# Halves of the last block, the first cast behind a high part, and an offset piece of attention in a hybrid decoder layer

## The chip, the cores and the metric

The kernel runs on one core of a Trainium2 chip. The metric is the device time in microseconds of one execution. The kernel before took 2251.83 us, the median of three runs (2251.02, 2251.83 and 2252.1). The engines are called PE (TensorE, matrix products; PEld is its weight load), ACT (ScalarE), DVE (VectorE), POOL (GpSimd) and SP (SyncE, which here issues most of the DMAs). "L417" is line 417 of the kernel before.

## The reference, cut to what matters

One layer on 256 tokens of width 2048: a SwiGLU feed-forward, a mixer of windowed attention beside RWKV-7 time mixing, a cross-attention into a memory, a second feed-forward, and a last RMS norm.

```
x = x + 0.5 * swiglu(rms_norm(x, ffn1_norm), ffn1_w_gate, ffn1_w_up, ffn1_w_down)
x = gated_parallel_mixer(x, mix_norm, w_in, sinks, ..., w_proj_attn, w_proj_rwkv, w_out)
x = memory_cross_attention(x, mem, cross_norm, mem_norm, w_q, w_kv, w_o)
x = x + 0.5 * swiglu(rms_norm(x, ffn2_norm), ffn2_w_gate, ffn2_w_up, ffn2_w_down)
return rms_norm(x, final_norm)

def rms_norm(x, g):          # mean over the 2048 columns of a token
    return x * rsqrt(mean(x * x) + 1e-6) * g
def swiglu(h, w_gate, w_up, w_down):
    return (silu(h @ w_gate) * (h @ w_up)) @ w_down
```

The windowed attention has 16 heads of 64 in 4 groups that share a key and a value head. The 256 tokens are two blocks of 128; the queries of a block see their own block and the one before it, within a window of 128. Each head has a sink, which takes part in the maximum and in the sum of the softmax alone.

## The kernel before, in words

All products are taken in about full float precision out of three passes in fp32r: an operand is divided into a high part (a cast on ACT) and a low part (the rest, a subtraction on DVE), and `times` (L414) adds high x high (L417), high x low (L418) and low x high (L419) in one PSUM bank. Weights come in units of 256 rows by 512 columns. `load` (L321) fetches them, through SP's queue but for one piece, `split_unit` (L338) casts (L344) and subtracts (L345), two units ahead of their use (`AHEAD`), in buffers of three.

Activations stand with features across partitions. `feat` (L598) transposes a block of token rows on PE into one of the two "tr" banks of PSUM (L605). `Norm.block` (L625) takes these transposes, multiplies them by the gain into the high part (ACT, L632) and makes the low part (DVE, L633). The factor of the norm is applied after the product. It is a square with a sum per token on ACT (L641, and L1528 for the last norm), then in `rstd` (L648) a reduction and a scaling on DVE (L651, L652) and a power on POOL (L654).

The order of the work is a list of generators, `Interleave` (L52). The main products run as plain loops (`product`, L395, and `product_pair`, L477), and after each piece of a product they call `bg.tick()`, which advances the background generators by one step each, at most `limit` of them in a group. So attention, norms and the RWKV chain are woven between the main products; `yield from idle(n)` lets n steps pass. What comes out is then put in an order for each engine by a scheduler of the framework, which may move an instruction past others where no dependency forbids it; `tc.issue_after(i)` adds an edge that keeps the instructions under it behind `i` on its engine.

**Start.** The rows of x and the first weights are issued at once; the very first weight is fetched in pieces. The first two units (u < AHEAD) are cast in halves, and `tc.issue_after(first.ins)` (L343) keeps these casts behind `first`, the copy of the first gain (L252, L265).

**Attention.** `attend(kv, qb)` (L835) is one piece: four query heads of one key head, and one block of 128 queries. It waits for the keys, makes four scores in two "mm" banks out of a ring of three (L844), scales and masks them on DVE (L850), takes the maximum (L857) and the sink, the exponentials on ACT with their sums (L869), the division on DVE (L877), transposes (L883) with copies to SBUF (L886), the product with the values (L891), and the two parts of the result (L898, L899). Scores and value products are fp32 products, which the trace records twice each. The eight pieces are put in the group "attn" (L905 to L907) in the order of kv, and of qb within it; two of the group advance at a time, the next one when one of them is done. So both blocks of a key head go in step. When the last piece is done, "attn" is set, and `decay_and_rate` (L946) starts behind it, then `removal_keys` (L1008), `substitute` (L1075), and the state's chain `pairs` (L1203) and `finish` (L1323), whose result is wanted by the product with `w_proj_rwkv` (L1398). Square roots (L1023) and the sigmoids of the gates (L1109) need different function tables on ACT.

**Tail.** The last down products of the second feed-forward are made one block of 512 columns at a time (L709 to L717). For block 3, `product(..., skew=True)` finishes the first 128 tokens some products before the others. Each result is added to x on DVE for all 512 columns (L713), then `done2` (L1525) squares and sums it on ACT (L1528) into column n of `ss`, a tile of four columns for each half of the tokens. For blocks 0 to 2, POOL multiplies by the final gain beforehand. Then, per token half, `rstd`, four scalings on ACT and DVE (L1542 to L1546) and three stores (L1549).

`aligned(sp)` (L734) takes a tile of 16 columns, "shift", at the start of each pool, and nothing uses it.

Of the kernel before, what the change touches and what calls it, by code (L numbers as in the profile page):

```python
# [7 lines left out]
F32 = mybir.dt.float32  # L8
F32R = mybir.dt.float32r
AF = mybir.ActivationFunctionType  # L10
ALU = mybir.AluOpType
# [4 lines left out]
P = 128  # L16
# [18 lines left out]
AHEAD, LOADED = 2, 4  # L35
# [97 lines left out]
def decoder_layer(ctx: ExitStack, tc: tile.TileContext, a: dict, out: bass.AP):  # L133
    nc = tc.nc
    act, dve, pool, pe = nc.scalar, nc.vector, nc.gpsimd, nc.tensor
# [4 lines left out]
    stat = ctx.enter_context(tc.tile_pool(name="stat", bufs=3))  # L140
# [23 lines left out]
    def wait_for(name):  # L164
        while name not in bg.seen:
            yield

    def idle(n):
        for _ in range(n):
            yield  # L170
# [91 lines left out]

    g_ffn1, fetch, fill = row_vectors(chunks(["ffn1_norm"], KD), "g_ffn1", act)
    fetch()
    first = fill()  # L265
    rows = chunks(["mix_norm", "cross_norm", "mem_norm", "ffn2_norm"], KD)
    gains, fetch_gains, fill_gains = row_vectors(rows, "gains", pool)
    g_mix, g_cross, g_mem, g_ffn2 = (gains[:, i * KD : (i + 1) * KD] for i in range(4))
# [69 lines left out]
    def split_unit(u, rows=slice(0, KU)):  # L338
        n, raw = units[u][3], raws[u]
        hi = wp.tile([P, KU, n], F32R, tag="hi", name="hi")  # L340
        lo = wp.tile([P, KU, n], F32R, tag="lo", name="lo")
        for s in (slice(0, 1), slice(1, 2)) if u < AHEAD else (rows,):
            with tc.issue_after(first.ins) if u < AHEAD else nullcontext():  # L343
                at["hi"] = act.copy(hi[:, s], raw[:, s])  # L344
            at["lo"] = dve.tensor_tensor(lo[:, s], raw[:, s], f32(hi[:, s]), ALU.subtract)  # L345
        return hi, lo
# [268 lines left out]
    class Norm:  # L615
# [9 lines left out]
        def block(self, n, src):  # L625

            for h in range(2):
                b = feat(src, [2 * h * P, (2 * h + 1) * P])
                for j in range(2):
                    c = 4 * n + 2 * h + j  # L630
                    g = self.gain[:, c : c + 1]
                    last = act.activation(self.x.at(0, c), b[:, j, :], AF.Copy, scale=g)  # L632
                    dve.scalar_tensor_tensor(  # L633
                        self.x.at(1, c), b[:, j, :], g, f32(self.x.at(0, c)),
                        ALU.mult, ALU.subtract,
                    )
                    self.x.done.add(c)
                yield
            with tc.issue_after(last.ins):
                for t in range(2):  # L640
                    act.activation(  # L641
                        junk_t[:], src[:, t, :], AF.Square, accum_out=self.ss[:, t, n : n + 1]
                    )
            if n == 3:
                yield
                self.r = rstd(self.ss[:])
# [11 lines left out]
    def feed_forward(sp, x, norm: Norm, wg, wu, wd, done, begin_last=lambda: None, last=False):  # L658
        if last:
            for tag, shape, dt, bufs in (  # L660
                ("hhi", [P, 16, T], F32R, 1), ("hlo", [P, 16, T], F32R, 1),
                ("hb", [P, 2, 512], F32, 2), ("thia", [P, KU, 512], F32R, 1),
                ("tloa", [P, KU, 512], F32R, 1), ("thib", [P, KU, 512], F32R, 1),
                ("tlob", [P, KU, 512], F32R, 1),
            ):
                sp.tile(shape, dt, tag=tag, name=tag, bufs=bufs)
        begun = at["item"]
        c = combinations(
            sp, norm.x, SEVEN, "c", lambda: norm.r is not None and at["item"] > begun + 4
        )  # L670
        c["next"] = []
        for gi, (j0, nj) in enumerate(GROUPS):
            h = Act(
                [sp.tile([P, 16, T], F32R, tag="hhi", name="hhi")],
                [sp.tile([P, 16, T], F32R, tag="hlo", name="hlo")], 16,
            )
            ch = combinations(sp, h, SEVEN_DOWN[nj < 4], "d", early=False)

            def transposed(hb, c):
                for q in range(2):  # L680
                    split(h, c + 2 * q, 2, feat(hb, [2 * q * P, (2 * q + 1) * P]))
                    yield

            for j in range(j0, j0 + nj):
                if j > 0:
                    hb = gate_and_up(sp, norm.x, c, norm.r, wg)

                    c["next"].append(transposed(hb, 4 * (j - j0)))
                    continue
                pg = product(norm.x, wg)  # L690
                hb = sp.tile([P, 2, 512], F32, tag="hb", name="hb", bufs=2)
                for t in range(2):
                    act.activation(hb[:, t, :], pg[t][:], AF.Silu, scale=norm.r[t])
                pu = product(norm.x, wu)
                for t in range(2):
                    dve.scalar_tensor_tensor(
                        hb[:, t, :], pu[t][:], norm.r[t], hb[:, t, :], ALU.mult, ALU.mult
                    )
                c["next"].append(transposed(hb, 0))
            end = gi == len(GROUPS) - 1  # L700
            bg.spawn("feat", c["next"].pop())
            if end:
                begin_last()

            def col(t, n):
                return x[:, t, n * 512 : (n + 1) * 512]

            for n in (0, 2):
                if last and end and n:  # L709
                    for m in (n, n + 1):  # L710
                        pd = product(h, wd, skew=m == 3)
                        for t in range(2):
                            dve.scalar_tensor_tensor(  # L713
                                col(t, m), pd[t][:], 0.5, col(t, m), ALU.mult, ALU.add
                            )
                        done(m)
                    continue  # L717
                down(sp, h, ch, wd, [[col(t, n + i) for i in range(2)] for t in range(2)])
                if end:
                    done(n)  # L720
                    done(n + 1)
# [11 lines left out]

    def aligned(sp):  # L734

        sp.tile([P, 16], F32, name="shift")


    with tc.tile_pool(name="f1", bufs=1, reuse_waits="tile") as sp:
# [4 lines left out]
        def col(n):  # L744
            return x[:, :, n * 512 : (n + 1) * 512]
# [26 lines left out]
    with tc.tile_pool(name="mx", bufs=1, reuse_waits="tile") as sp:  # L772
# [61 lines left out]

        def attend(kv, qb):  # L835
            yield from wait_for("kv")
            w = P * (qb + 1)
            tq = slice(qb * P, qb * P + P)
            s = t4("s", (P, 2, 2, T))
# [656 lines left out]


    with tc.tile_pool(name="f2", bufs=1, reuse_waits="tile") as sp:
        aligned(sp)
        at["pool"] = sp  # L1500
        x = sp.tile([P, 2, D], F32, name="x")
        fins = []

        def fin(n):

            return fins[n // 2][:, n % 2]

        def gain():
            for n in range(4):
                if n % 2 == 0:  # L1510
                    fins.append(wp.tile([P, KU, 512], F32, tag="raw", name="raw", bufs=4))
                cb = slice(n * 512, (n + 1) * 512)
                pool.dma_start(fin(n), a["final_norm"][cb].unsqueeze(0).broadcast_to([P, 512]))
                yield

        def reload():
            for n in range(4):
                cb = slice(n * 512, (n + 1) * 512)
                yield from idle(20)
                pool.dma_start(x[:, :, cb], blk(x3d, n))  # L1520

        bg.spawn("const", reload())
        ss = stat.tile([P, 2, 4], F32, tag="ss", name="ss")

        def done2(n):  # L1525
            for t in range(2):
                xs = x[:, t, n * 512 : (n + 1) * 512]
                act.activation(junk_t[:], xs, AF.Square, accum_out=ss[:, t, n : n + 1])  # L1528
                if n < 3:
                    pool.tensor_tensor(xs, xs, fin(n), ALU.mult)  # L1530

        feed_forward(
            sp, x, n4, W["ffn2_w_gate"], W["ffn2_w_up"], W["ffn2_w_down"], done2,
            begin_last=lambda: bg.spawn("const", gain()), last=True,
        )
        for t in range(2):
            r = rstd(ss[:, t : t + 1, :])[0]
            for n in range(4):
                cb = slice(n * 512, (n + 1) * 512)
                xs = x[:, t, cb]  # L1540
                if n == 3:
                    dve.scalar_tensor_tensor(xs, xs, r, fin(n), ALU.mult, ALU.mult)  # L1542
                elif n == 1:
                    dve.tensor_scalar(xs, xs, r, None, ALU.mult)
                else:
                    act.activation(xs, xs, AF.Copy, scale=r)  # L1546
            for cb, queue in ((slice(0, 1024), nc.sync), (slice(1024, 1536), act),
                              (slice(1536, 2048), nc.sync)):
                queue.dma_start(out[0, t * P : (t + 1) * P, cb], x[:, t, cb])  # L1549
# [30 lines left out]
```

## Time and profile before

| | us |
|---|---|
| median of three runs | 2251.83 |
| the profiled execution | 2252.57 |
| its span, first to last instruction | 2250.8 |
| PE idle in the span | 15.6 |
| ACT busy | 1226.5 |
| DVE busy | 1782.0 |

The profile is one execution. A row of its timeline gives the start, the duration, the engine, the line and the operation, what it writes and reads, and how many were merged (x2); in square brackets the engine's idle time ahead of it and what ended it. Products are pipelined on PE, so the time between two starts tells more than a duration. A row of the waits gives the engine and the line that waited, for whom, the sum, the number of times and the longest.

### The profile page before, as it was taken

Reading aid. Unit: us, or ns where it says so; the run is one execution under the profiler, and the core shown is the slowest. Engines: PE = TensorE matmul, PEld = TensorE weight load, DVE = VectorE, ACT = ScalarE, POOL = GpSimd, SP = SyncE. Lnnn points to the kernel's source line nnn. Section 1 sums busy time; section 2 is a strip of 40 time slices with the busy share of each in tenths; the row PEclk is TensorE's granted clock in tenths of the full one; section 3 lists DMA queues with packets and bytes.
Section 4 is the critical chain, followed back from the end, with each engine's and each line's share of the span. In section 5 each row is a group of like instructions: output and inputs, shape, how many; then the busy total and the mean of one; then the engine's idle time right before and its main releaser. Section 6 shows DMA issues by size and latency. Waiting matters only on the chain.

```text
span 2250.8 us, 28046 instructions
## 1 busy us (share of the span) xinstructions
PE 2235.2 (99%) x10617; PEld 1840.3 (82%) x10617; DVE 1782.0 (79%) x2279; ACT 1226.5 (54%) x1601; POOL 132.6 (6%) x192
## 2 busy tenths in 40 slices
PE   9999999999999999999999999999999999999998
PEld 7888888888888877788888888888888888888886
DVE  7898988998989476887534566557998988998987
ACT  6555555555556467444444446556555555554554
POOL 1000000000001000301220040001000000000002
PEclk9999999999999999999999999999999999999999
DMA  7555555556556544676523476548565565555564
GB/s 263 187 201 201 197 203 202 193 190 216 192 188 205 163 142 150 201 223 212 166 77 109 163 261 227 186 159 284 185 213 187 195 210 194 190 209 200 189 207 147
DMA packets 219143, 432.49 MB, mean 192 GB/s; under 512 B 14107, under 2 KB 16384, under 8 KB 219008
## 3 DMA queue, kind: packets, MB, share of 16 engines
q1 hardware_dynamic: 210432, 404.78, 53.3%
q0 software_dynamic: 8112, 25.12, 3.5%
q8 instruction: 83, 1.36, 0.2%
q10 hardware_dynamic: 464, 0.79, 0.1%
q14 instruction: 52, 0.43, 0.1%
HBM read 417.56 MB, written 13.11 MB: 191 GB/s over the span
## 4 chain that ended last, share of the span: by engine, by line
PE 94%; DVE 3%; DMA 1%; issue 1%; POOL 1%; ACT 0%; SPq 0%; POOLq 0%; DVEq 0%; ACTq 0%
PE acc L417 19%; PE acc L418 19%; PE acc L419 19%; PE mm L419 8%; PE mm L418 8%; PE mm L417 8%; PE tr L605 2%; PE tr L418 2%; PE tr L419 2%; PE tr L417 2%; PE mm L1254 1%; DVE lo L345 1%; PE tr L1190 1%; DMA raw<-in_w_out_dram 0%; PE mm L844 0%
## 5 line engine op out<-in xcount | busy, mean ns | idle before, releaser
L345 DVE TENSOR_TENSOR lo<-raw,hi 128x1024 fp32r<-128x1024 f32 (+1 forms) x770 | 894.5, 1163 | 336.6 <-ACT hi L344 334.4
L344 ACT CAST hi<-raw 128x1024 fp32r<-128x1024 f32 (+1 forms) x770 | 759.3, 997 | 734.7 <-PE acc L419 519.6
L417 PE MATMUL acc<-hi,xhi 128*128 128x512 f32 (+1 forms) x1196 | 474.3, 397 | 2.4 <-ACT xhi L632 1.9
L418 PE MATMUL acc<-lo,xhi 128*128 128x512 f32 (+1 forms) x1196 | 464.8, 389 | 0.0
L419 PE MATMUL acc<-hi,xlo 128*128 128x512 f32 (+1 forms) x1196 | 464.1, 388 | 0.0
L417 PEld LDWEIGHTS acc<-hi,xhi 128*128 128x128 f32 x1196 | 225.0, 188 | 51.4 <-issue 4.0
L419 PEld LDWEIGHTS acc<-hi,xlo 128*128 128x128 f32 x1196 | 224.5, 188 | 46.9 <-DVE xlo L633 1.0
L418 PEld LDWEIGHTS acc<-lo,xhi 128*128 128x128 f32 x1196 | 224.9, 188 | 45.3 <-issue 1.7
L352 ACT CAST thi<-raw 128x1024 fp32r<-128x1024 f32 x172 | 178.9, 1050 | 60.4 <-DVE raw L373 46.5
L353 DVE TENSOR_TENSOR tlo<-raw,thi 128x1024 fp32r<-128x1024 f32 x172 | 208.3, 1220 | 0.7 <-ACT thi L352 0.4
L417 PE MATMUL mm<-hi,xhi 128*128 128x512 f32 x380 | 149.3, 393 | 0.0
L419 PE MATMUL mm<-hi,xlo 128*128 128x512 f32 x380 | 148.2, 390 | 0.0
L418 PE MATMUL mm<-lo,xhi 128*128 128x512 f32 x380 | 148.2, 390 | 0.0
L418 PE MATMUL acc<-lo,hhi 128*128 128x512 f32 x372 | 145.6, 391 | 0.8 <-DVE lo L345 0.8
L419 PE MATMUL acc<-hi,hlo 128*128 128x512 f32 x372 | 145.6, 391 | 0.0
L417 PE MATMUL acc<-hi,hhi 128*128 128x512 f32 x372 | 144.9, 390 | 0.0
L419 PEld LDWEIGHTS mm<-hi,xlo 128*128 128x128 f32 x380 | 71.3, 188 | 14.8
L418 PEld LDWEIGHTS mm<-lo,xhi 128*128 128x128 f32 x380 | 71.4, 188 | 14.5
L417 PEld LDWEIGHTS mm<-hi,xhi 128*128 128x128 f32 x380 | 71.4, 188 | 14.5
L418 PEld LDWEIGHTS acc<-lo,hhi 128*128 128x128 f32 x372 | 69.9, 188 | 15.5 <-DVE lo L345 1.2
L417 PEld LDWEIGHTS acc<-hi,hhi 128*128 128x128 f32 x372 | 69.9, 188 | 14.3
L419 PEld LDWEIGHTS acc<-hi,hlo 128*128 128x128 f32 x372 | 69.9, 188 | 14.0
(392 smaller groups left out, 3511.9 us busy)
## 6 DMA issues: line engine op xcount, KB each, us to landing
raw<-in_ffn_w_up_dram SPq DMA_DIRECT2D x88, 1024.0 KB, 5.4
raw<-in_ffn_w_down_dram SPq DMA_DIRECT2D x88, 1024.0 KB, 5.1
raw<-in_ffn_w_gate_dram SPq DMA_DIRECT2D x84, 1024.0 KB, 5.1
raw<-in_w_in_dram SPq DMA_DIRECT2D x136, 512.0 KB, 3.5
raw<-in_w_out_dram SPq DMA_DIRECT2D x32, 512.0 KB, 4.5
raw<-in_w_proj_attn_dram SPq DMA_DIRECT2D x16, 512.0 KB, 3.9
raw<-in_w_proj_rwkv_dram SPq DMA_DIRECT2D x16, 512.0 KB, 5.7
raw<-in_w_cross_kv_dram SPq DMA_DIRECT2D x16, 512.0 KB, 3.6
```

The source lines that it names most:

```text
L344: at["hi"] = act.copy(hi[:, s], raw[:, s])
L345: at["lo"] = dve.tensor_tensor(lo[:, s], raw[:, s], f32(hi[:, s]), ALU.subtract)
L352: act.copy(hi[:], v[:])
L353: dve.tensor_tensor(lo[:], v[:], f32(hi[:]), ALU.subtract)
L417: pe.matmul(o, xh, hi, start=first, stop=False, **how)
L418: pe.matmul(o, xh, lo, start=False, stop=False, **how)
L419: pe.matmul(o, xl, hi, start=False, stop=last, **how)
L605: pe.transpose(b[:, o : o + P], tok[:, t, col : col + P], ident[:])
L1190: pe.matmul(b[e][:, o : o + P], x1[r, j, cs_], x2[r, j, cs_], start=True, stop=True)
L1254: pe.matmul(vb[:, (o + k) * P : (o + k + 1) * P][:, r], lhs(k, e), rhs[:, k, r], start=first and k + e == 0, stop=True, **ek,)
```

## The change

There are three edits.

1. The casts of the first two weight units are kept behind the first high part of x (`at["xhi"]`, set by the first `Norm.block`) and no longer behind the copy of the gain.
2. `attend(0, 1)` lets four steps pass before it begins. Since two pieces advance at a time and each piece is followed by the next of the list, the second lane of the attention stands four steps behind the first from there on.
3. In the last block the addition is made in two halves of 256 columns for each half of the tokens, and each half is squared at once: the first on ACT as before, the second on DVE, by an operation that multiplies and sums. The sums go to five columns, which now lie in the tile "shift" (called `room`); the fifth takes the sum of DVE.

```diff
-    first = fill()
+    fill()
...
-            with tc.issue_after(first.ins) if u < AHEAD else nullcontext():
+            with tc.issue_after(at["xhi"].ins) if u < AHEAD else nullcontext():
...
                     last = act.activation(self.x.at(0, c), b[:, j, :], AF.Copy, scale=g)
+                    at.setdefault("xhi", last)
...
                 if last and end and n:
+
+                    whole = [(t, slice(0, 512)) for t in range(2)]
+                    parts_ = [(t, slice(c, c + 256)) for t in range(2) for c in (0, 256)]
+                    pieces = {2: whole, 3: parts_}
                     for m in (n, n + 1):
                         pd = product(h, wd, skew=m == 3)
-                        for t in range(2):
+                        for t, cs in pieces[m]:
                             dve.scalar_tensor_tensor(
-                                col(t, m), pd[t][:], 0.5, col(t, m), ALU.mult, ALU.add
+                                col(t, m)[:, cs], pd[t][:, cs], 0.5, col(t, m)[:, cs],
+                                ALU.mult, ALU.add,
                             )
-                        done(m)
+                            done(m, t, cs)
...
-        sp.tile([P, 16], F32, name="shift")
+        return sp.tile([P, 16], F32, name="shift")
...
             yield from wait_for("kv")
+            if kv == 0 and qb:
+                yield from idle(4)
...
-        aligned(sp)
+        room = aligned(sp)
...
-        ss = stat.tile([P, 2, 4], F32, tag="ss", name="ss")
-
-        def done2(n):
-            for t in range(2):
-                xs = x[:, t, n * 512 : (n + 1) * 512]
-                act.activation(junk_t[:], xs, AF.Square, accum_out=ss[:, t, n : n + 1])
+        ss = room[:, :10].rearrange("p (t n) -> p t n", t=2)
+
+        def done2(n, t=None, cs=slice(0, 512)):
+            for t in range(2) if t is None else (t,):
+                xs = x[:, t, n * 512 : (n + 1) * 512][:, cs]
+                if cs.start:
+                    dve.scalar_tensor_tensor(
+                        junk_t[:, cs], xs, 1.0, xs, ALU.mult, ALU.mult, accum_out=ss[:, t, 4:5]
+                    )
+                else:
+                    act.activation(
+                        junk_t[:, cs], xs, AF.Square, accum_out=ss[:, t, n : n + 1]
+                    )
                 if n < 3:
                     pool.tensor_tensor(xs, xs, fin(n), ALU.mult)
```

## The prediction

> **What bounds the kernel now.** I read the page's span and its chain of waits first, then the busy times by stretch, then what TensorE (PE) waits for.
>
> ```profile
> span 2250.8 us, 28046 instructions
> PE 2235.2 (99%) x10617; PEld 1840.3 (82%) x10617; DVE 1782.0 (79%) x2279; ACT 1226.5 (54%) x1601; POOL 132.6 (6%) x192
> PE 94%; DVE 3%; DMA 1%; issue 1%; POOL 1%; ACT 0%; SPq 0%; POOLq 0%; DVEq 0%; ACTq 0%
> ...
> 0.00:25.00 25.00, 22.02 (x103) 17.58 (x104) 12.78 (x20) 16.37 (x32) 1.14 (x11) 1.00 0.94 337
> 2230.00:2251.00 21.00, 12.33 (x55) 9.89 (x53) 8.60 (x13) 6.22 (x10) 1.89 (x3) 0.87 0.26 100
> ```
>
> The rows by stretch give the stretch, its length, then the busy time of PE, weight load, DVE, ACT and POOL. PE is busy for 2235.2 of 2250.8 us, and 94% of the chain that ended last is PE. Its idle time is 15.6 us in all: 3.0 (25.00-22.02) in the first 25 us, 8.7 (21.00-12.33) in the last 21, and some 4 between. The three edits sit in just these places (start, attention around 787 to 850, tail). The diff takes no matmul away, so even a perfect result could not win more than a few us; nearly all of those 8.7 and 3.0 us are load and store latency that no edit touches.
>
> The profiled execution took 2252.57 us, 1.77 outside its span; the median of the three shown is 2251.83, so 0.74 is taken off a sum made against the profiled one.
>
> **Start: the first cast goes behind a high part.**
>
> ```profile
> 5.44 1.47 PE L605 MATMUL tr<-ident,x 128*128 128x128 f32 x8
> 6.88 0.62 ACT L344 CAST hi<-raw 128x512 fp32r<-128x512 f32 x1 [1.20 <-DMA raw<-in_ffn_w_gate_dram]
> 7.41 0.47 ACT L632 ACTIVATE xhi<-tr,g_ffn 128x256 fp32r<-128x256 f32 x1
> ...
> 7.92 0.19 PEld L417 LDWEIGHTS acc<-hi,xhi 128*128 128x128 f32 x1 [1.26 <-ACT xhi L632]
> ...
> 10.86 1.04 ACT L344 CAST hi<-raw 128x1024 fp32r<-128x1024 f32 x1 [1.08 <-DMA raw<-in_ffn_w_gate_dram]
> 12.33 0.50 PE L417 MATMUL acc<-hi,xhi 128*128 128x512 f32 x1 [0.91 <-ACT xhi L632]
> ```
>
> ScalarE (ACT) waits 1.20 us for the weights to land at 6.88, casts them, and only then makes the first high part, for which PE waits until 7.92. In the new order the high part comes first, inside those 1.20 us: all eight transposes are issued by 6.91 and four of them are enough for it; I put their end near 6.2, half of 1.47 behind 5.44, and its own 0.47 (L632 writes 256 columns) fits before or just behind 6.88. The cast starts at 6.88 and ends at 7.50, so the first matmul can start near 7.54: 0.4 earlier than 7.92. But what is late next is already in the trace. After its first twelve products PE waits again until 12.33, for a high part that stands on ACT behind the cast of the second weight, and this cast waits for a DMA that lands at 10.86. In the built order these two stand exactly where they stood, and the DMAs before them are the same. The 0.4 us turn into a longer wait at 12.33: I take **0**, with ends -0.4 and 0. The added wait (the cast behind the high part) holds casts and their subtractions queued on ACT and VectorE (DVE); the DMA covers it.
>
> **Attention: one piece four steps behind.** Two pieces of the attention run beside the main products, one for each 128-row block. Before, both are issued in the same step; now the second is offset by four steps, and as later pieces follow in the two lanes, the offset stays.
>
> ```profile
> PE tr L605 <- ACT tok L788: 0.8, 1, 0.8
> PE tr L605 <- DVE yalo L899: 0.3, 1, 0.3
> PE mm L844 <- DVE s L850: 0.2, 1, 0.2
> ...
> 815.01 0.40 PE L419 MATMUL acc<-hi,xlo 128*128 128x512 f32 x1
> 816.16 0.33 PE L605 MATMUL tr<-ident,tok 128*128 128x128 f32 x1 [0.75 <-ACT tok L788]
> ...
> 821.21 0.40 PE L419 MATMUL acc<-hi,xlo 128*128 128x512 f32 x1
> 821.88 0.44 PE L605 MATMUL tr<-ident,tok 128*128 128x128 f32 x2 [0.27 <-DVE yalo L899]
> ```
>
> Those are all the waits of PE between 780 and 870. Read by starts (a main product follows its forerunner by 0.23 us, below), the first two hold PE 1.15-0.23 = 0.92 and 0.67-0.23 = 0.44 us; with the 0.2 of the third that is 1.56. All come of both pieces standing together: four score products want a fourth PSUM buffer of a ring of three; a transpose wants a token tile whose scaling stands on ACT behind three copies of both pieces. Spread out, the pieces ask for two buffers at a time. I take **-1.4**: the first and third wait go, some 0.15 of the second is left. Ends: 0 (waits reappear elsewhere) and -1.56.
>
> What spreading costs is seen where an fp32 run breaks into the main products (fp32r):
>
> ```profile
> 856.56 0.39 PE L418 MATMUL acc<-lo,xhi 128*128 128x512 f32 x1
> 856.78 0.39 PE L419 MATMUL acc<-hi,xlo 128*128 128x512 f32 x1
> 857.10 1.13 PE L964 MATMUL mm<-xs,wa 64*128 64x256 f32 x8
> 858.16 0.50 PE L417 MATMUL acc<-hi,xhi 128*128 128x512 f32 x1
> 858.50 0.40 PE L418 MATMUL acc<-lo,xhi 128*128 128x512 f32 x1
> ...
> 795.70 0.71 PE L844 MATMUL mm<-kd,qt 64*128 64x128 f32 x6
> 796.34 0.44 PE L883 MATMUL tr<-ident,s 128*128 128x128 f32 x2
> 796.71 0.48 PE L844 MATMUL mm<-kd,qt 64*128 64x128 f32 x2
> 797.12 0.44 PE L883 MATMUL tr<-ident,s 128*128 128x128 f32 x2
> ```
>
> Main products start 0.23 apart; the one ahead of the fp32 run takes 0.32, the one behind it 0.34: 0.20 for going in and out. Inside the run there may be as much again: one fp32 matmul (two records) alone takes 797.12-796.71 = 0.41, in a run of three 0.64/3 = 0.21. In the built order the fp32 runs rise from 77 to 84, since pieces that stood together now stand apart, and the mixer steps behind the attention shift with them. Seven more at 0.20 are **+1.4**. Ends: 0 (runs broken by transposes alone, as the second fence shows, may already pay this) and 7 x 0.40 = +2.8.
>
> The end of the attention, and with it decay, removal keys, substitution and the chain of the state, come later by up to some tens of instructions. On SyncE's queue (SP) the four loads of the triangular blocks (L1080) move behind three weight loads; on GpSimd's (POOL) the loads of L950 and L951 pass one subtraction, and the gate stores (L1113) change places with the block stores (L1070). No DMA is added. Who needs the end of it is far off:
>
> ```profile
> L611 DVE TENSOR_TENSOR yrlo<-yq,yrhi x4: 684/686/693, 1186.0 to 1273.0; 128x512 fp32r<-128x512 f32 x4
> ...
> L417 PEld LDWEIGHTS acc<-hi,yrhi x64: 187/188/190, 1293.1 to 1338.8; 128*128 128x128 f32 x64
> ```
>
> The last part is ready by 1273.7 and used at 1293.1: 19.4 us. In the built order the last chain matmul stands 24 main products later, 24 x 0.23 = 5.5 us. **0**; without that cover the price is what it is late by.
>
> ACT gets two more table loads (19 for 17), since square roots now fall on both sides of a gate's sigmoid.
>
> ```profile
> 888.95 1.28 ACT L1023 ACT_TABLE_LOAD   x1
> 890.24 0.60 ACT L1023 ACTIVATE sq<-tr 128x512 f32<-128x512 f32 x1
> 891.51 1.05 ACT L344 CAST hi<-raw 128x1024 fp32r<-128x1024 f32 x1 [0.67 <-PE acc L419]
> 894.23 1.05 ACT L344 CAST hi<-raw 128x1024 fp32r<-128x1024 f32 x1 [1.67 <-PE acc L419]
> ```
>
> Behind such a load on ACT wait the casts of the weights, and behind these PE. A cast is due every 2.72 us, when PE leaves a buffer of three, so its result is wanted two units (5.44 us) later; cast (1.05) and subtraction (1.23, below) leave about 3.1 us. The densest place issues sigmoid, load, root, load, sigmoid: 0.63+1.28+0.60+1.28+0.63 = 4.4 us, and begins about 2 us before the next cast is due. So it is some 2.4 late of 3.1: **0**. Ends: 0 and 2 x 1.28 = +2.6.
>
> [...]
>
> **Tail: the last block in halves.**
>
> ```profile
> 2242.37 0.69 DVE L713 SCALAR_TENSOR_TENSOR x<-acc,x 128x512 f32<-128x512 f32 x1 [0.30 <-PE acc L419]
> 2243.09 0.63 ACT L1528 ACTIVATE junk<-x 128x512 bf16<-128x512 f32 x1 [0.84 <-DVE x L713]
> 2243.63 0.19 ACT L1528 ACTIVATION_READ_ACCUMULATOR junk<-x 128x1 f32 x1
> 2243.84 0.16 DVE L651 TENSOR_REDUCE ms<-ss 128x1 f32<-128x4 f32 x1 [0.79 <-ACT junk L1528]
> 2244.04 0.15 DVE L652 TENSOR_SCALAR ms<-ms 128x1 f32<-128x1 f32 x1
> ...
> 14.61 0.87 DVE L633 SCALAR_TENSOR_TENSOR xlo<-tr,g_ffn,xhi 128x256 fp32r<-128x256 f32 x2
> 11.94 1.23 DVE L345 TENSOR_TENSOR lo<-raw,hi 128x1024 fp32r<-128x1024 f32 x1 [1.12 <-ACT hi L344]
> ```
>
> Only the second token half is on the path; the first is done while PE works on. Before, from the addition's start to the reduction: 2243.84-2242.37 = 1.47 us. After, DVE adds two halves (0.87 for two of 256 columns by L633) and then squares the second half itself (0.87-0.39 = 0.48 alone), with a dependent hand-over of 0.04 on either side as from L651 to L652: 1.43. ACT's half square ends earlier and is hidden. **0** (-0.04): the square that left ACT came to stand on DVE behind two additions. The reduction over five columns for four costs nothing visible. No row shows DVE adding up a square: ends -0.2 (no hand-overs, each step 0.39) and +0.15, if its sum has to be read by an instruction of its own as ACT's is (0.19).
>
> [...]
>
> **The sum:** 0 - 1.4 + 1.4 + 0 + 0 + 0 = 0 against 2252.57, so 2252.57 - 0.74 = 2251.8.
>
> **Rivals.**
> - *Waits go, switches are free* (faster). If the extra fp32 runs only replace switches that the bunched pieces paid between themselves, the 1.56 go whole, and start and tail add up to 0.6 (0.4 and 0.2): 2251.8-2.2 = 2249.6. For it: at 796 short runs already stand alone among transposes. Against: seven more runs in the order.
> - *Switching outweighs* (slower than before). Place: the seven added runs from 787 on; price 0.40 each, 2.8 against 1.4 won: 2253.2, and 2254.6 if no wait goes. It decides from 0.20 a run. The 0.41 for a matmul alone speaks for it.
> [...]
> - *It doesn't do what it says*: the start's gain is taken back at 12.33. That is in the forecast.
>
> **How the numbers follow.** About 0.2% (4.5 us) is what a measurement of this kernel can tell from no change; 2251.83 less or plus that is 2247.3 and 2256.3. Forecast (2250.6 to 2253.0) 0.55; faster rival (down to 2249) 0.19; switching 0.18; ACT's loads 0.05, half of it beyond 2256.3; 0.03 for a gain beyond 2247.3, which needs waits that no edit here touches. So faster 0.03, same 0.94, slower 0.03. The range takes the forecast, most of the faster rival and switching with no wait gone: 2249.2 to 2254.6.
>
> **What would show it.** Start: first matmul near 7.54 and the wait before about 12.33 longer by as much. Attention: the three waits above gone from PE's list, main products beside the added fp32 runs at 0.32 and 0.34. Tail: 1.4 to 1.5 us from the last addition's start to the reduction. I am wrong if PE starts waiting for casts (L344) or subtractions (L345) between 860 and 960, if the state's chain is late at 1293, or if the second matmul wait in the start moves with the first.

## The result, and the profile after

The changed kernel takes 2256.48 us, the median of 20 runs (2253.77 to 2258.03), against 2251.81 for the kernel before in as many runs (2251.02 to 2253.03). The ratio is 1.002, with a 95% interval of 1.0014 to 1.0026: 4.7 us slower. The forecast was 2251.8 and its range ended at 2254.6, so it was wrong on the slow side. The profiled execution of the changed kernel took 2255.28 us, 1.2 less than the median. Lines behind the edits are 8 higher than before (L1059 is now L1067, L964 is L972, L844 is L852); L713 is L718, and L1528 is L1541.

The top of the page of the changed kernel:

```profile
span 2253.2 us, 28054 instructions
PE 2238.0 (99%) x10617; PEld 1840.7 (82%) x10617; DVE 1787.0 (79%) x2285; ACT 1228.8 (55%) x1603; POOL 134.6 (6%) x192
PE 96%; DVE 1%; issue 1%; DMA 1%; ACT 1%; POOL 0%; POOLq 0%; ACTq 0%; DVEq 0%
```

PE runs as many matmuls as before (x10617), is busy for 2.8 us longer (2238.0 against 2235.2), and the span is 2.4 longer. So by this profile the loss isn't idle time: the same matmuls take more of PE's time. The stretches (start and end, length, then busy PE, PEld, DVE, ACT, POOL; the granted clock stands before the last two numbers) show two places, the first from the changed kernel, the second from it too, and the third from the kernel before:

```profile
0.00:25.00 25.00, 22.48 (x103) 17.87 (x104) 12.80 (x20) 16.42 (x32) 1.15 (x11) 0.93 0.94 337
...
920.00:1000.00 80.00, 78.29 (x356) 62.92 (x354) 64.25 (x89) 35.84 (x38) 15.56 (x12) 0.98 0.71 217
```

```profile
920.00:1000.00 80.00, 79.99 (x369) 65.01 (x368) 63.34 (x93) 35.63 (x36) 10.48 (x9) 1.00 0.73 228
```

Between 920 and 1000 PE gets through 356 matmuls in place of 369, is idle for 1.71 us in place of 0.01, and its clock is 0.98 on average. In the trace's clock records it is 0.5 for 3.41 us, from 960.20 to 963.61, and for as long in the start, from 7.88 to 11.29; before, it was 1.0 in both places. The window in the start doesn't come of the first edit: the profiles of five kernels without that edit have one there too, and those of the first edit alone and of both edits without the offset have none.

What PE waits for between 780 and 1300, in the changed kernel:

```profile
PE mm L1067 <- DVE lt L1073: 1.0, 1, 1.0
PE mm L972 <- DMA wa<-in_rwkv_w_dram: 1.0, 1, 1.0
PE acc L417 <- ACT hi L344: 0.7, 1, 0.7
PE tr L605 <- DVE mk L1204: 0.6, 1, 0.6
```

Besides the three waits of the attention (tok, yalo, s), the kernel before has these three in the same stretch:

```profile
PE acc L417 <- DVE ga L1112: 0.4, 1, 0.4
PE tr L1190 <- DVE mk L1196: 0.3, 1, 0.3
PE mm L1059 <- DVE lt L1065: 0.3, 1, 0.3
```

The three waits of the attention are gone, as forecast. In their place stand the first three rows of the changed kernel, all of them behind the attention, at 959, 857 and 945 (lt is the copy of the removal keys' products out of their PSUM banks; the wait for it has grown from 0.3 to 1.0). Here is the one for wa, in the changed kernel's timeline; two rows of POOL stand above it:

```profile
850.11 2.37 POOL L927 TENSOR_TENSOR d<-p 128x512 f32<-128x512 f32 x1 [1.09 <-ACT p L924]
...
854.09 0.59 POOL L958 DMA_DIRECT2D wa<-in_rwkv_w_dram  x1 [0.48 <-issue]
```

```profile
857.75 1.13 PE L972 MATMUL mm<-xs,wa 64*128 64x256 f32 x4 [0.95 <-DMA wa<-in_rwkv_w_dram]
858.81 0.50 PE L417 MATMUL acc<-hi,xhi 128*128 128x512 f32 x1
859.24 1.13 PE L972 MATMUL mm<-xs,wa 64*128 64x256 f32 x4
860.30 0.50 PE L418 MATMUL acc<-lo,xhi 128*128 128x512 f32 x1
```

Compare the row that the prediction shows from before: `857.10 1.13 PE L964 ... x8`. There eight records took 1.13 us. Now four take 1.13, and the other four 1.13 again. `64*128` is the weight's shape: these products use 64 of the array's 128 rows. The tile wa has one factor in its lower and one in its upper 64 rows, and where a lower product stands next to an upper one, both run at once. In the trace of before their starts are 0.007 us apart (857.101 and 857.108). Here the lower ones went alone, a main product came between, and the upper ones paid the whole time a second time. The row from before is its second run of these products. Its first was split as well, at less cost: one product stood ahead of the rest, with work of the attention between.

```profile
850.85 0.70 PE L964 MATMUL mm<-xs,wa 64*128 64x256 f32 x2
...
853.08 1.13 PE L964 MATMUL mm<-xs,wa 64*128 64x256 f32 x6
```

The same happens in the removal keys (`mm<-kk,at`), in the changed kernel and then in the one before:

```profile
954.87 1.16 PE L1067 MATMUL mm<-kk,at 64*128 64x128 f32 x16
955.96 0.51 PE L419 MATMUL acc<-hi,xlo 128*128 128x512 f32 x1
956.39 1.16 PE L1067 MATMUL mm<-kk,at 64*128 64x128 f32 x8
...
959.47 1.44 PE L1067 MATMUL mm<-kk,at 64*128 64x128 f32 x8 [1.03 <-DVE lt L1073]
...
961.44 0.63 PE L418 MATMUL acc<-lo,xhi 128*128 128x512 f32 x1
961.86 0.63 PE L419 MATMUL acc<-hi,xlo 128*128 128x512 f32 x1
```

```profile
945.39 1.16 PE L1059 MATMUL mm<-kk,at 64*128 64x128 f32 x16
...
947.83 1.65 PE L1059 MATMUL mm<-kk,at 64*128 64x128 f32 x16
```

Sixteen records in pairs take 1.16 us; eight of one half take 1.16 too. In PE's order there were four runs of 8 products (16 records each) before, and there are runs of 12, 4, 8, 4 and 4 after. The last two rows from the changed kernel show the slow clock: main products 0.42 apart in place of 0.23.

### The profile page after: what moved, and what is told of

It is laid out like the page before. It is cut to its first block, busy times and chain, and to the rows that moved or that the text cites. A ratio compares the mean times of both kernels' runs of the same rounds, so it can differ in the third digit from the quotient of the medians.

```text
span 2253.2 us, 28054 instructions
## 1 busy us (share of the span) xinstructions
PE 2238.0 (99%) x10617; PEld 1840.7 (82%) x10617; DVE 1787.0 (79%) x2285; ACT 1228.8 (55%) x1603; POOL 134.6 (6%) x192
## 4 chain that ended last, share of the span: by engine, by line
PE 96%; DVE 1%; issue 1%; DMA 1%; ACT 1%; POOL 0%; POOLq 0%; ACTq 0%; DVEq 0%
PE acc L417 20%; PE acc L418 19%; PE acc L419 19%; PE mm L419 8%; PE mm L418 8%; PE mm L417 8%; PE tr L605 2%; PE tr L418 2%; PE tr L417 2%; PE tr L419 2%; PE mm L1262 1%; PE tr L1198 1%; DMA raw<-in_w_out_dram 0%; PE mm L852 0%; DVE lo L345 0%
```

## The experiments

All times are medians, each beside the kernel before on the same chip. First, one edit at a time.

**The offset alone** (the four lines of edit 2, nothing else).

> Only the second edit: attend(0, 1) begins four steps later; start and tail as before. Theory A (the offset's followers): the offset moves the steps behind the attention so that PE waits three times (about 1.0 for wa near 858, 0.7 for a cast near 945, 1.0 for lt near 959) and then loses part of a clock window (3.41 us at half speed, some 1.7); against that the 1.56 won near 800. So it bears the whole loss: 2255 to 2257 us, with single runs spread over 3 to 4 us. [...] Theory C (switching alone, my rival): 1.4 to 2.8 us less the waits won, 2252 to 2254.6, with runs as close together as those of before (2 us).

Measured: 2255.95 us against 2252.05, ratio 1.0018 (1.0009 to 1.0027), runs from 2254.77 to 2258.35. Of the 4.7 us, 3.9 are here, and the intervals of the two ratios overlap. Its trace has the same four waits as the changed kernel.

**The first edit alone**, with `issue_after(at["xhi"].ins)`.

> Only the first edit: the first casts stand behind the first high part. Theory A: nothing to see, 2251.5 to 2252.2, since the product waits for its next high part near 12.4 in any case. Theory B: a half-speed window at 7.9 to 11.3 costs 1 to 2 us, 2253 to 2254.

Measured: 2251.66 us, ratio 0.9999 (0.999 to 1.0008). Nothing to see.

**The third edit alone**.

> Only the third edit: the last block is added and squared in halves. By the changed kernel's trace the stretch from the last addition to the reduction is 1.33 us against 1.47. Theory A and B: 0.1 less, 2251.6 to 2251.8, too little to tell. A loss here of over 1 us would mean that neither holds.

Measured: 2252.37 us, ratio 1.0002 (0.9993 to 1.0011). Nothing to see.

**Both, without the offset**.

> The first and third edit without the offset of the attention. Theory A: 2251.4 to 2252.0, no worse than before, and runs as close together as before's. Theory B: 2253 to 2254.

Measured: 2252.3 us, ratio 1.0001 (0.9992 to 1.001). Theory B, the start, falls: no kernel without the offset is slower than before by more than the measurement tells.

Then, what about the offset costs.

**Everything behind the attention four steps later, the attention as before**:

```diff
             yield from wait_for("attn")
+            yield from idle(4)
             wa = t4("wa", (P, RW))
```

> Start, attention and tail as before, both pieces of the attention in step; but decay_and_rate lets four steps pass after the attention has ended, so that everything behind it (removal keys, substitution) stands four steps later. Theory A (the loss lies in where the followers fall, not in the pieces apart): most of the loss shows here too, 2253.5 to 2256, with a new wait for lt or a cast between 930 and 970 and runs spread over more than 2 us. Theory C (switching of the pieces set apart): as before, 2251.8 to 2252.4.

Measured: 2254.55 us, ratio 1.0013 (1.0005 to 1.0022). So 2.4 of the 3.9 us come with both pieces of the attention still in step. Its waits between 780 and 1300 have the two forecast rows:

```profile
PE mm L1060 <- DVE lt L1066: 1.0, 1, 1.0
...
PE acc L417 <- ACT hi L344: 0.7, 1, 0.7
```

Its trace has the removal keys in runs of 12, 4, 8, 4 and 4 products, like the changed kernel.

**The offset with wa fetched earlier**:

```diff
             yield from wait_for("small")
-            yield from wait_for("attn")
             wa = t4("wa", (P, RW))
             pool.dma_start(wa[0:64, :], W["rwkv_w2"])
             pool.dma_start(wa[64:128, :], W["rwkv_a2"])
+            yield from wait_for("attn")
```

> The offset alone, with wa fetched before the attention has ended and not behind it. The wait of 1.0 us for that load near 858 goes. Theory A: 0.5 to 1.0 us less than the offset alone (2255.95), 2255.0 to 2255.5; the two waits and the half-speed window near 945 to 964 stay. Theory C: the wait is not what costs, 2255.9.

Measured: 2252.21 us, 3.7 less than the offset alone; I had expected 0.5 to 1.0. The loads are issued at 819.29 now. The wait was only part of the price, as this row shows: the products are one run again.

```profile
857.06 1.14 PE L966 MATMUL mm<-xs,wa 64*128 64x256 f32 x8
```

Between 780 and 860 this kernel gains 2.2 us on the offset alone, 0.95 for the wait and the rest for the second run and its way in and out. Another 1.6 came between 959 and 964: the profiled run here has no half-speed window there, though it still waits 1.0 for lt.

**The offset with a transpose bank for the removal keys**:

```diff
                 lt = t4("lt", (P, 8, P))
-                b = [mm() for _ in range(2)]
+                b = [mm(), tr() if c else mm()]
```

> The offset alone, with one bank of the second block of the removal keys' products taken from the two transpose banks, so that the third group of these products need not wait until lt is taken out of the ring of three. Theory A: the wait of 1.0 us near 959 goes, and with it most of the half-speed windows of 3.41 us that follow it; 1.5 to 2.5 us less than the offset alone, 2253.5 to 2254.5, with runs within 2 us of each other. If the clock has nothing to do with the wait: 0.7 to 1.0 less, and windows of half speed near 960 still there in about half of the runs.

Measured: 2251.35 us, 4.6 less than the offset alone, and I had expected 1.5 to 2.5. Again the pairs: with a bank for each half there is no split run and no wait for lt. The two halves now stand in two kinds of banks (mm and tr), and their records alternate:

```profile
955.08 0.37 PE L1061 MATMUL mm<-kk,at 64*128 64x128 f32 x1
955.08 0.37 PE L1061 MATMUL tr<-kk,at 64*128 64x128 f32 x1
```

On the way to 960 PE gains about 3.8 us on the offset alone, and 1.3 more by 965 for the window that didn't come; behind it 0.6 is lost again, where PE now waits 0.3 for a subtraction. This mend takes away the wait and the split together, so it doesn't tell them apart.

**An offset of three**, `idle(3)`.

> The offset alone, but of three steps in place of four. In the built order ACT has 15 table loads here against 17 before and 19 with four steps. Theory A (where the followers fall decides): not between before and four steps by the size of the offset, but by its own waits; without table loads ahead of the casts near 940 the cast is not late: 2252 to 2254. Theory C (pieces apart): 2255 to 2256, like four steps.

Measured: 2260.88 us, ratio 1.004 (1.0027 to 1.0052): my expectation missed by 7 us. Fewer table loads didn't save the casts. Its trace, the rows of PE and one of ACT:

```profile
858.88 1.13 PE L966 MATMUL mm<-xs,wa 64*128 64x256 f32 x4 [1.21 <-DMA wa<-in_rwkv_w_dram]
861.65 1.13 PE L966 MATMUL mm<-xs,wa 64*128 64x256 f32 x4 [0.29 <-DMA wa<-in_rwkv_a_dram]
...
978.97 0.73 PE L417 MATMUL acc<-hi,yahi 128*128 128x512 f32 x2 [1.71 <-ACT hi L344]
```

```profile
977.88 2.93 ACT L344 CAST hi<-raw 128x1024 fp32r<-128x1024 f32 x3
```

wa is late and split as with four steps. Three casts stood on ACT behind the two sigmoids of a gate, the second of which waited for its product until 977.29; PE then waited 1.71 for the first of them. That is only a part of the price: by the account of the next section, whose table leaves this kernel out, wa costs 2.3 more than before, the main products 3.1 (with this wait), the value products 1.5 and the rest 1.4. A smaller offset isn't a smaller cost; each has its own collisions.

**The pairs by themselves.** In the kernel before, the four products of the lower rows first, then the four of the upper:

```diff
-                for j in range(4):
-                    for e in range(2):
+                for e in range(2):
+                    with tc.issue_after(upper.ins) if e else nullcontext():
+                        for j in range(4):
...
+                    upper = m
```

> The kernel before, with one thing changed: in the removal keys' products (L1059) all four of the lower 64 rows are issued first and the four of the upper 64 rows behind them, in place of in turn. Same products, same four runs, no wait added. Theory D (the halves of the array): two products of 64 rows run at once on the two halves of the array when they stand next to each other (their starts are 0.007 us apart in the trace), so a run of four pairs takes the 1.09 us of a run of four single ones; set apart, each of the four runs is 0.67 to 0.89 longer: 2.7 to 3.5 in all, 2254.8 to 2255.7 us. Rival (only the waits and the breaks in the main products cost): 2251.9 to 2252.3, as before.

Measured: 2253.49 us against 2252.06, ratio 1.0007 (0.9998 to 1.0016): 1.4 longer, against 2.7 to 3.5 expected. The direction is that of theory D, but the interval still touches no change, so the trace has to carry it. One of the four runs:

```profile
945.78 1.68 PE L1060 MATMUL mm<-kk,at 64*128 64x128 f32 x16
```

It is 0.52 us longer than the 1.16 in pairs, not 0.67 to 0.89: the first upper product began 0.53 us behind the first lower one (946.303 and 945.778), beside the third of the four. And two of the four runs were long before, since a wait for lt stood in them (the 1.65 at 947.83 above is one). So 0.9 us went into these products, and most of the rest is a second wait of 0.4 for ga. That a run pays for its halves apart shows in this trace; the whole time a second time was seen where something stood in between, a main product or a wait, as at 858 and 956.

**Both mends.** The offset with wa earlier and the transpose bank:

> The offset alone, with both mends: wa fetched before the attention has ended, and one bank of the second block of removal keys from the transpose banks. Theory A with D (the offset wins in the attention itself, and loses by the pairs that it splits, the waits with them and the clock windows behind them): by the account of PE's time both losses go, 2.3 for wa and 3.8 for the removal keys, and about 1 of clock: 2248.5 to 2250, faster than before. If the gains of the two single mends are the same one, seen twice: 2251.3 to 2252.

Measured: 2248.87 us (2248.61 to 2249.49), ratio 0.9986 (0.9978 to 0.9995), 3.2 us faster than before. What PE still waits for between 780 and 1300:

```profile
PE acc L417 <- ACT hi L344: 0.7, 1, 0.7
PE tr L605 <- DVE mk L1198: 0.6, 1, 0.6
PE acc L418 <- DVE lo L345: 0.3, 1, 0.3
```

**The mends without the offset**:

> The kernel before with the same two mends and no offset. Theory D: of the removal keys' 6.5 us of PE some 1.7 go (4.8 in the mended bank), nothing is won at wa, which was in time: 2250.2 to 2250.8. If the offset wins nothing, this is as fast as the mended offset.

Measured: 2250.23 us, ratio 0.9992 (0.9983 to 1.0001). The interval just touches no change; by the account below it is the bank that is worth some 1.8 us to the kernel before as well, and wa adds nothing. The offset adds 1.4 on top, once its followers are mended: the slowest run with it (2249.49) is faster than the fastest without (2249.73).

**The whole change with both mends**:

> The changed kernel whole (start, offset, tail) with both mends. Start and tail have shown no difference alone, so as the mended offset within 0.4 us: 2248.5 to 2250.3, and some 6 to 7 us less than the changed kernel.

Measured: 2249.29 us, ratio 0.9987 (0.9979 to 0.9996): 7.2 less than the change as it was made. The mended offset alone (2248.87) is the best of all; start and tail add nothing to it.

## Where the time went

For each kernel's profiled run I added up, between 770 and 1300 us, what PE spent from start to start, less the 0.227 us of a main product of 512 columns (0.133 for one of 288), and gave the time just before and behind a run to the run. Removal keys in a transpose bank (`tr<-kk,at`) are counted with the others. Differences from the kernel before, in us:

| | late4 | offset alone | wa earlier | transpose bank | both mends | mends, no offset |
|---|---|---|---|---|---|---|
| scores (kd,qt) | 0.0 | -0.9 | -0.9 | -0.9 | -0.9 | 0.0 |
| transposes (s, tok) | +0.7 | -0.8 | -0.8 | -0.8 | -0.8 | -0.5 |
| value products (pt,vt) | +0.1 | +1.1 | +1.1 | +1.1 | +1.1 | 0.0 |
| wa | 0.0 | +1.7 | -0.6 | +1.5 | -0.6 | 0.0 |
| removal keys (kk,at) | +2.0 | +2.1 | +2.0 | -1.7 | -1.7 | -1.3 |
| among main products | +0.3 | +1.9 | +0.4 | +1.0 | +1.0 | -0.1 |
| the rest | -1.0 | -1.0 | -1.0 | -1.0 | -1.1 | 0.0 |
| sum | +2.0 | +4.0 | +0.1 | -0.8 | -2.9 | -1.9 |
| median against before | +2.4 | +3.9 | 0.0 | -0.8 | -3.2 | -1.8 |

The sums follow the medians to 0.4 us, though each is of one execution; that of "late4" was the fastest of its eleven (2253.75). "Among main products" holds the wait of 0.7 for a cast, less one of 0.4 for ga that goes, and in the offset alone some 1.6 for the half-speed window. That window near 960 is in both profiled runs of the unmended offset of four and in none of the others here. The single runs fit: those of the offset alone spread by 3.6 us, and the three of eleven with a mean clock of 0.999, like most of before's, lie at 2254.8; the two of the changed kernel with 0.999 are its two fastest (2253.77 and 2254.22). So of the 3.9 us about 1.2 seem to be the clock. The mean doesn't tell a window near 960 from one in the start, which a wait swallows, so this is an estimate. What brings on the half speed near 960 stays open: "late4" and "wa earlier" wait 1.0 us for lt as well, and their profiled runs have no window there.

## Why the prediction was wrong, by its steps

- **Start, 0: right in size, and for the reason given.** The first matmul started at 7.66 (forecast 7.54, 7.93 before), the second point at 12.42 (12.33). The run of the first edit alone shows it without a half-speed window: 7.61 and 12.39, with a wait at the second point of 1.14 in place of 0.91. The gain was swallowed there, as said. The half-speed window from 7.88 to 11.29 in the changed kernel's profile stretched the twelve products and was swallowed by the same wait.
- **Three waits go, -1.4: right, and too small.** They went. Scores and transposes together got 1.7 us cheaper.
- **Switches, +1.4: the right order of size.** It was the value products that paid, 1.1, their runs being split from five to eight. By the trace there were more breaks than the seven counted: main products are broken into 112 times between 780 and 1300 against 97 before, so the price of one was lower, and that the size fits is in part luck. The second fence of that step was misread, too. Of the three score products at 795.70 two ran side by side (starts at 795.701 and 795.707), while the one at 796.71 is a half without its partner. So the step from 0.21 to 0.41 is for the most part a split pair, and not the break. With the gain above the attention itself won 0.6 us, not 0, and the steps of the chain behind it another 1.0 ("the rest", in "late4" too).
- **"Attention ends later ... 0": the step that failed.** I looked for cover only where the state's chain ends (19.4 us at 1293), and that cover did hold. But the steps just behind the attention have none. I named the loads of wa passing a subtraction on POOL and put no price on it: they were issued at 825.20 before and at 854.09 after, 3.7 us ahead of their use. And the removal keys, four steps later, met the ring of three banks so that one half of a pair waited for lt. The runs show +1.7 and +2.1 for these two, and the whole loss is gone when both are mended. Behind the second came the half-speed window, some 1.6 in the profile, for which the sum had no term. That these products run in pairs could be seen in the trace of before (two starts 0.007 us apart), and the split runs in the built order; I read the quoted row of L964 for the way in and out alone.
- **ACT's table loads, 0: not settled.** A wait for a cast came. The densest place has three loads where I counted two, and 5.8 us pass from the first to the casts, in place of 4.4:

```profile
936.46 1.28 ACT L1117 ACT_TABLE_LOAD   x1
937.76 0.69 ACT L1117 ACTIVATE ga<-acc,rs 128x512 f32<-128x512 f32 x1
938.46 1.28 ACT L1031 ACT_TABLE_LOAD   x1
...
940.37 1.28 ACT L1117 ACT_TABLE_LOAD   x1
...
942.25 1.98 ACT L344 CAST hi<-raw 128x1024 fp32r<-128x1024 f32 x2
944.46 1.05 ACT L344 CAST hi<-raw 128x1024 fp32r<-128x1024 f32 x1 [0.22 <-PE acc L419]
```

```profile
940.85 3.37 DVE L1035 RECIPROCAL sq<-sq 128x256 f32<-128x256 f32 x2
944.13 2.29 DVE L345 TENSOR_TENSOR lo<-raw,hi 128x1024 fp32r<-128x1024 f32 x2
```

```profile
945.55 0.50 PE L417 MATMUL acc<-hi,xhi 128*128 128x512 f32 x1 [0.68 <-ACT hi L344]
```

  PE waits for the cast at 944.46, and this one began 0.22 us after ACT had nothing left to do, when PE freed its buffer: no load held this cast. The two casts behind the loads were in time (the first ends at 943.29, its product starts at 944.26). What is late is a subtraction, behind two reciprocals on DVE (3.37 us); PE's order has a product of a later unit (`hi,xhi` among `yahi`) in the place of the one that needs it. So the 0.7 is again a follower that fell elsewhere, which "late4" has too. But the loads have a share in the late subtraction. The reciprocals waited for the root, which ACT began at 939.76 behind its loads, though the root's product on PE had ended at about 937.6; before, no load stood ahead of the root there, and a subtraction went between the two reciprocals. What would be left of the 0.7 without the loads no run shows. A load held ACT for no longer than its own 1.28 us in these rows: behind each of the three the next operation starts 0.02 us after the load's end (936.46 + 1.28, and 937.76).
- **Tail, 0: right in sum, by two terms.** From the last addition to the reduction 1.33 us (1.43 forecast, 1.47 before):

```profile
2244.89 0.76 DVE L718 SCALAR_TENSOR_TENSOR x<-acc,x 128x256 f32<-128x256 f32 x2 [0.50 <-PE acc L419]
...
2245.68 0.42 DVE L1537 SCALAR_TENSOR_TENSOR junk<-x 128x256 bf16<-128x256 f32 x1
2246.03 0.08 DVE L1537 DVE_READ_ACCUMULATOR junk<-x 128x1 f32 x1
2246.22 0.16 DVE L652 TENSOR_REDUCE ms<-shift 128x1 f32<-128x5 f32 x1
```

  The sum is read by an instruction of its own (DVE_READ_ACCUMULATOR, 2246.03), at 0.08 and not at the 0.19 of ACT. But in the profiled runs the time outside the span is 2.06 to 2.08 us in all four kernels that hold the third edit and 1.70 to 1.75 in all others: what the tail wins is lost there.
- **The sum** was 0 against +4.7. One of the signs that were to prove me wrong came, a wait for a cast between 860 and 960, but it is only 0.7 of the loss. The two dear places, wa and the removal keys, were not on the list.

## What to carry to other kernels

When a step is moved, price its followers, not only the last user: for each one look at what its loads, its buffers and its partner in a pair were ready for. In these traces products on 64 rows are cheap only in pairs; count in the built order how many runs hold both halves, for a run of one half costs as much as a run of both (1.16 us for eight records of the removal keys' products of one half, 1.16 for sixteen of both). A change that loses in this way may still hold a gain, which shows when the collisions are mended one at a time.

## What the runs showed of the hardware that was not expected

- The clock of PE fell to half for 3.41 us (960.20 to 963.61 in the changed kernel) behind a wait of 1.03 us beside 64-row products, the longest of PE between 940 and 960. The half-speed window in the start of that profile is as long (7.88 to 11.29). The length of a wait alone doesn't decide: behind the one of 1.71 us with `idle(3)` no half-speed window followed (the clock was 1.00 from 960 to 1000).
- Upper and lower 64-row products overlap also where four stand behind four, but only from 0.53 us on, beside the third and the fourth of the lower ones (946.303 and 945.778 with the halves issued apart; the run took 1.68 us, against 1.16 in pairs).
- The time outside the span grew by some 0.35 us with the third edit (2.06 to 2.08 us, against 1.70 to 1.75 without it); no view of the trace shows on what.
